# A graph-attention kernel: one-hot transposes folded into the gather matmul, wider blocks, paired results, and a first block spread by TensorE

## The chip, the cores and the metric

The kernel runs on one core of one Trainium2 chip. The metric is the device time of one execution in microseconds; a profiled execution also gives a span, which is about 2 us shorter than its time. PE is TensorE, DVE is VectorE, ACT is ScalarE, POOL is GpSimd, SP is SyncE, which here only issues memory transfers.

## The reference, cut to what matters

There are 4096 nodes with 64 features, 50000 edges, and 4 heads of 64 outputs.

```python
for h in range(n_heads):
    x_proj[h] = x @ weight[h]
# per edge: score = leaky_relu(x_proj[src].att_src + x_proj[dst].att_dst), slope 0.2
output[h, dst] += np.exp(edge_scores[h, i]) * x_proj[h, src]
# per destination: divide by (sum of exp over its edges + 1e-8)
```

## The kernel before

It first sorts the edges, twice, on DVE, so that the edges of each block of 121 destinations lie together as 16 groups of up to 128. Then it loops over 34 blocks. In each block it builds one-hots of the destination and of the source from broadcast bins, gathers features and scores with one-hot matmuls, transposes the destination one-hots on PE, weighs the features by the exponentials, sums them per destination with matmuls, and projects and divides. Names in the lines below: `bc` is the broadcast bins, `oh` the one-hots, `xps` or `ps` what the gather leaves in PSUM (the memory that matmuls write), `ex` the exponentials, `xs` the copied features, `wv` the weights, `val` the weighted features, `acc` the sums, `aT` their copy, `pf` the projection, `inv` and `res` the division. The parts that the change touches:

```python
BD = 121
...
def gather(self, b):                       # per group t of 16
    T.matmul(out=o, lhsT=oh[:, 1, e], rhs=xa[:, 2 * t, :], ...)            # 72 columns
    T.matmul(out=o, lhsT=oh[:, 2, e], rhs=xa[:, 2 * t + 1, :], ...)        # 72 columns
    T.matmul(out=o[:, Din:XC], lhsT=oh[:, 0, e], rhs=adb[:, b, :], ...)    # 8 columns
    ...
    S.activation(out=ex, in_=xps, func=ACTF.Exp);  S.copy(out=xs[:], in_=xps[:, :, 0:Din])

def turn(self, b):                         # 16 transposes and two copies
    T.transpose(out=sp[:, i, :], in_=oh[:, 0, t * W2:(t + 1) * W2], identity=identb[:])
    S.copy(out=Sb[:, q * NT // 2:(q + 1) * NT // 2, :], in_=sp[:])

def run(self):
    ...
    for b in range(ND):
        self.load(b + 3)                   # 1 MB of broadcast bins, SP queue
        self.weigh(b, ...)                 # DVE: wv, val
        self.gather(b + 1)
        self.turn(b + 1)
        self.onehot(b + 2)                 # DVE
        if b:
            self.sink.give(b - 1)          # PE: project; DVE: inv, res; SP: store
        self.scatter(b)                    # PE: 16 + 32 sums
...
win.unpack(0, nc.sync, nc.scalar)          # DVE: bins of 8 blocks; stored to memory
for b in range(3):
    blocks.load(b)                         # and read back, broadcast
for i in range(1, NI):
    win.unpack(i, nc.scalar, nc.scalar)
blocks.run()
```

## Time and profile before

| stage of the profiled execution (span 314.9 us) | us |
|---|---|
| start to the first unpack instruction (sorts, mostly DVE) | 0 to 121.99 |
| first block: unpack, memory, one-hots, gather | 121.99 to 138.01 |
| first val to last val, 33 steps, 4.93 each in the mean | 138.01 to 300.61 |
| last val to the end of the last res | 300.61 to 306.67 |
| to the end (last stores land) | 306.67 to 314.9 |

The median of the first runs was 317.16 us. Two conventions for reading: one *val* instruction is one block, so the distance between starts of consecutive vals is the loop's period; and the name in square brackets behind a line is what the profile takes to have ended the idle time before it. That name is inferred.

### The profile page before, as it was taken

How to read it: one execution, taken by the hardware profiler on the slowest of the kernel's cores; microseconds unless marked ns; L12 is line 12 of the kernel's file. 1: busy time of each engine (PE TensorE's matmuls, PEld its weight loads, DVE VectorE, ACT ScalarE, POOL GpSimd, SP SyncE). 2: the span in 40 equal slices, each digit the busy share in tenths (PEclk: the TensorE clock that was granted, in tenths of full speed). 3: DMA queues.
4: the chain of work that ended last, by engine and by line, in shares of the span. 5: the costliest groups of instructions: out<-in, count | busy, mean ns of one | idle time of the engine just before them, and what ended most of it. 6: DMA issues, size and time to landing. Idle time of an engine off the chain costs nothing. (4 is left out here: it accounts for less than half of the span.)

```text
span 314.9 us, 9697 instructions
## 1 busy us (share of the span) xinstructions
PE 207.2 (66%) x4122; PEld 202.2 (64%) x4122; DVE 275.9 (88%) x552; ACT 172.9 (55%) x324; POOL 18.6 (6%) x40
## 2 busy tenths in 40 slices
PE   0049999000000000099999999999999999999970
PEld 0027999000000000099999999999999999999970
DVE  8999999993999995479999999999999999999960
ACT  3984000000999600067777768677686767768640
POOL 6800000002000005000000000000000000000000
PEclk9999555555555555579999999999999999999996
DMA  7200000002000002991865857667575766667110
GB/s 206 46 1 0 2 0 0 1 0 67 1 0 0 0 28 51 300 395 32 284 234 224 290 191 271 216 237 251 204 276 191 258 228 253 232 227 272 56 38 21
DMA packets 13551, 43.97 MB, mean 140 GB/s; under 512 B 3308, under 2 KB 8492, under 8 KB 9148
## 3 DMA queue, kind: packets, MB, share of 16 engines
q1 hardware_dynamic: 11332, 41.92, 37.7%
q10 hardware_dynamic: 1464, 0.70, 0.8%
q0 software_dynamic: 704, 0.66, 0.8%
q8 instruction: 34, 0.56, 0.8%
q14 instruction: 17, 0.14, 0.2%
HBM read 38.22 MB, written 5.05 MB: 137 GB/s over the span
## 5 line engine op out<-in xcount | busy, mean ns | idle before, releaser
L449 DVE TENSOR_TENSOR val<-xs,wv 128x4096 bf16<-128x4096 bf16 (+1 forms) x35 | 78.0, 2231 | 4.1 <-ACT xs L423 0.7
L437 ACT COPY Sb<-sp 128x1024 bf16<-128x1024 bf16 x68 | 66.3, 1039 | 0.0
L413 PE MATMUL xps<-xa,oh 128*128 128x72 bf16 x544 | 54.1, 194 | 14.5 <-DVE oh L401 14.5
L463 PE MATMUL acc<-Sb,val 128*128 128x121 bf16 x1088 | 63.6, 217 | 0.0
L413 PEld LDWEIGHTS <-oh 128*128 128x128 bf16 x544 | 50.4, 98 | 13.9 <-DVE oh L400 13.9
L463 PEld LDWEIGHTS <-val 128*128 128x128 bf16 x1088 | 58.5, 98 | 0.1
L415 PE MATMUL xps<-xa,oh 128*128 128x72 bf16 x544 | 53.7, 195 | 0.1
L417 PE MATMUL xps<-adb,oh 128*128 128x8 bf16 x544 | 52.8, 169 | 0.0
L415 PEld LDWEIGHTS <-oh 128*128 128x128 bf16 x544 | 49.4, 96 | 1.2 <-DVE oh L401 1.1
L417 PEld LDWEIGHTS <-oh 128*128 128x128 bf16 x544 | 50.1, 97 | 0.0
L400 DVE TENSOR_SCALAR oh<-bc,pF 128x4096 bf16<-128x4096 bf16 x34 | 43.5, 1281 | 4.6 <-DMA bc<-gat_bins 4.6
L420 ACT ACTIVATE ex<-xps 128x256 bf16<-128x256 f32 x34 | 13.4, 395 | 58.3 <-PE xps L417 58.3
L188 DVE TENSOR_TENSOR sA<-sB 128x256 f32<-128x256 f32 (+2 forms) x108 | 39.6, 408 | 1.8
L250 ACT ACTIVATE junk<-kr,nb 128x512 f32<-128x512 f32 x34 | 24.5, 722 | 25.6 <-DVE kr L301 24.5
L188 DVE TENSOR_TENSOR sB<-sA 128x256 f32<-128x256 f32 (+2 forms) x100 | 36.7, 408 | 1.7
L261 PE MATMUL cnt_ps<-sgn,sel 128*128 128x17 f32 (+1 forms) x6 | 1.7, 390 | 53.1 <-ACT sgn L253 53.1
L436 PE MATMUL sp<-identb,oh 128*128 128x128 bf16 x544 | 36.5, 221 | 0.0
L261 PEld LDWEIGHTS cnt_ps<-sgn,sel 128*128 128x128 f32 x6 | 1.4, 318 | 53.2 <-issue 53.2
L423 ACT CAST xs<-xps 128x1024 bf16<-128x1024 f32 x34 | 34.1, 1003 | 0.0
L436 PEld LDWEIGHTS <-oh 128*128 128x128 bf16 x544 | 31.4, 99 | 0.0
L401 DVE TENSOR_SCALAR oh<-bc,pF 128x2048 bf16<-128x2048 bf16 x34 | 25.4, 747 | 0.0
L345 PEld LDWEIGHTS at_ps<-uv,xT 64*128 64x128 f32 x132 | 25.1, 297 | 0.4 <-issue 0.4
(116 smaller groups left out, 255.7 us busy)
## 6 DMA issues: line engine op xcount, KB each, us to landing
bc<-gat_bins SPq DMA_DIRECT2D x34, 1024.0 KB
out_dram<-res SPq DMA_DIRECT2D x33, 121.0 KB
gat_sorted<-sA SPq DMA_DIRECT2D x2, 256.0 KB
eS<-in_edge_index_dram SPq DMA_DIRECT2D x1, 390.0 KB
eD<-in_edge_index_dram ACTq DMA_DIRECT2D x1, 390.0 KB
gat_bins<-tb ACTq DMA_DIRECT2D x9, 32.0 KB
out_dram<-res SPq DMA_DIRECT2D x1, 103.0 KB
win<-gat_sorted,wi POOLq DMA_INDIRECT x5, 2.6
```

The source lines that it names most:

```text
L188: V.tensor_tensor(out=av(d[:], o, [2 * h, n], [1, h]), in0=av(s[:], 0, [2 * h, n], [1, h]), in1=av(s[:], h, [2 * h, n], [1, h]), op=op)
L345: T.matmul(out=ps[:, b, :], lhsT=xT[:, b * step:b * step + P], rhs=uv[:, k, :], start=(b == 0), stop=True, skip_group_check=True)
L400: V.tensor_scalar(out=oh[:, 0:2, :], in0=bc[:], scalar1=pF[:, 0:1], scalar2=None, op0=OP.is_equal)
L401: V.tensor_scalar(out=oh[:, 2, :], in0=bc[:, 1, :], scalar1=pF[:, 1:2], scalar2=None, op0=OP.is_equal)
L413: T.matmul(out=o, lhsT=oh[:, 1, e], rhs=xa[:, 2 * t, :], start=(t % 4 == 0), stop=False, skip_group_check=True)
L415: T.matmul(out=o, lhsT=oh[:, 2, e], rhs=xa[:, 2 * t + 1, :], start=False, stop=False, skip_group_check=True)
L417: T.matmul(out=o[:, Din:XC], lhsT=oh[:, 0, e], rhs=adb[:, b, :], start=False, stop=True, skip_group_check=True)
L423: S.copy(out=xs[:], in_=xps[:, :, 0:Din])
L436: T.transpose(out=sp[:, i, :], in_=oh[:, 0, t * W2:(t + 1) * W2], identity=identb[:])
L437: S.copy(out=Sb[:, q * NT // 2:(q + 1) * NT // 2, :], in_=sp[:])
L449: V.tensor_tensor(out=av(val[:], h * Dout, [Dout, n], [C, NT], [1, Din]), in0=av(xs[:], 0, [0, n], [2, NT * Din // 2], [1, 2]), in1=av(wv[ ...
L463: T.matmul(out=acc[:, k * BD:(k + 1) * BD], lhsT=val[:, t, k * P:(k + 1) * P], rhs=Sb[:, t, 0:BD], start=False, stop=(t == NT - 1), skip_g ...
```

## The change

The intent is to relieve both full engines of the loop and to shorten the gap before it. The 16 transposes go: the third gather matmul gets the identity beside the scores as its moving side, so that it also delivers the turned one-hot, and the gather is done in three chunks (6, 6 and 4 groups) in two PSUM buffers. Blocks grow to 125 destinations, so 33 instead of 34. Epsilon is added by three tiny matmuls. Results are projected per block but divided and stored for two blocks at a time. The first block's bins are spread over the partitions by PE rather than through memory, and groups 3 and 4 are unpacked later.

```diff
-BD = 121
+BD = 125
-    eps = cst.tile([P, 1], F32)
-    V.memset(eps[:], 1e-8)
+    V.memset(e0[:], 1e-8)
+    V.memset(one[:], 1.0)
+    V.memset(nil[:], 0.0)
+    for i in range(3):                     # epsilon in three bf16 parts
+        V.tensor_copy(out=eps[:, i, :], in_=e0[:])
+        if i < 2:
+            V.tensor_copy(out=e1[:], in_=eps[:, i, :])
+            V.tensor_tensor(out=e0[:], in0=e0[:], in1=e1[:], op=OP.subtract)
 ... (cut: identity copied into adb, table layout)
+        def spread(self, b, tb): ...       # PE broadcasts the bins; ACT, ACT, DVE copy them out
-        def turn(self, b): ...
 ... (cut: gather(b, c) of one chunk:)
-                T.matmul(out=o[:, Din:XC], lhsT=oh[:, 0, e], rhs=adb[:, b, :], ...)
+                T.matmul(out=ps[:, i, 0:S0], lhsT=oh[:, 0, e], rhs=adb[:, b, :], ...)   # 136 columns
+            S.activation(out=..., in_=..., func=ACTF.Exp)
+            copy(out=xs[:, t0:t0 + n, 0:P + XC], in_=ps[:, 0:n, 0:P + XC])
 ... (cut: run)
                 self.load(b + 3)
                 self.weigh(b, 2 if b == ND - 1 else 1)
-                self.gather(b + 1)
-                self.turn(b + 1)
+                self.gather(b + 1, 0)
                 self.onehot(b + 2)
                 if b:
-                    self.sink.give(b - 1)
-                self.scatter(b)
+                    self.sink.project(b - 1)
+                    if b % 2 == 0:
+                        self.sink.give(b - 2, 2)     # inv, res and two stores
+                self.sums(b, -1)
+                self.gather(b + 1, 1)
+                self.sums(b, 0)
+                self.gather(b + 1, 2)
+                self.sums(b, 1)
 ... (cut: start)
-        for b in range(3):
+        for i in (1, 2):
+            win.unpack(i, nc.sync, nc.sync)
+        blocks.spread(0, win.tb[:, 0])
+        for b in range(1, 3):
             blocks.load(b)
-        for i in range(1, NI):
-            win.unpack(i, nc.scalar, nc.scalar)
-        blocks.run()
+        blocks.run([lambda i=i: win.unpack(i, nc.sync, nc.sync) for i in range(3, NI)])
```

More of the change, by code (lines that the diff above doesn't have):

```diff
@@ L110 @@
     pm8 = bits("pm8", 0, 7)
-    eps = cst.tile([P, 1], F32)
-    V.memset(eps[:], 1e-8)
+    e0 = cst.tile([1, H], F32)
+    e1 = cst.tile([1, H], F32)
+    eps = cst.tile([1, 3, H], BF16)
+    one = cst.tile([1, P], BF16)
+    nil = cst.tile([1, 3, H], BF16)
+    V.memset(e0[:], 1e-8)
[6 more added lines that the diff above has]
+            V.tensor_tensor(out=e0[:], in0=e0[:], in1=e1[:], op=OP.subtract)
     goff = cst.tile([P, 1], F32)
@@ L150 @@
     xa = cst.tile([P, NB, XC], BF16)
-    adb = cst.tile([P, ND, 2 * H], BF16)
+    AB = P + 2 * H
+    adb = cst.tile([P, ND, AB], BF16)
     Wbd = cst.tile([P, 2, P], F32)
@@ L333, in tables @@
             S.copy(out=uv[:, :, 2 * i:2 * i + 2], in_=av(ps2[:], 0, [2, 2], [1, 2]))
-        S.copy(out=xa[:, :, 0:Din], in_=xf[:])
+        S.copy(out=xa[:, :, 2 * H:XC], in_=xf[:])
         xT = pr.tile([Din, ND * BD + P - BD], F32)
@@ L341, in tables @@
             S.copy(out=xT[:, 4 * q * P:4 * (q + 1) * P], in_=ps[:])
-        for k, (n, step, to) in enumerate(((NB, P, xa[:, :, Din:XC]), (ND, BD, adb[:]))):
+        for k, (n, step, to) in enumerate(((NB, P, xa[:, :, 0:2 * H]), (ND, BD, adb[:, :, P:AB]))):
             ps = pp1.tile([P, n, H], F32, name=f"at_ps{k}")
@@ L348, in tables @@
             S.mul(out=to[:, :, H:2 * H], in_=ps[:], mul=ALPHA)
+        S.copy(out=adb[:, :, 0:P], in_=av(identb[:], 0, [0, ND], [1, P]))
     NT = NR
@@ L374, in unpack @@
                               in_=self.tb[:, i, k, :])
+    CH = ((0, 6), (6, 6), (12, 4))
+    S0 = P + 2 * H
+    XW = 256
     class Blocks:
@@ L382, in __init__ @@
             self.bp = pool(name="blk", bufs=2)
-            self.psx = pool(name="ps_x", bufs=1, space=PSUM)
-            self.pss = pool(name="ps_s", bufs=2, space=PSUM)
+            self.psx = pool(name="ps_x", bufs=2, space=PSUM)
             self.psa = pool(name="ps_a", bufs=1, space=PSUM)
             self.sink = sink
-            self.bc, self.oh, self.xps, self.ex, self.xs, self.wv, self.Sb, self.val = ({} for _ in range(8))
+            self.bc, self.oh, self.ex, self.xs, self.wv, self.val = ({} for _ in range(6))
         def load(self, b):
@@ L394, in load, with spread, onehot, gather @@
                 self.bc[b] = t
-        def onehot(self, b):
-            if b < ND:
-                bc = self.bc.pop(b)
-                oh = self.bp.tile([P, 3, NT * W2], BF16, name="oh")
-                V.tensor_scalar(out=oh[:, 0:2, :], in0=bc[:], scalar1=pF[:, 0:1], scalar2=None, op0=OP.is_equal)
-                V.tensor_scalar(out=oh[:, 2, :], in0=bc[:, 1, :], scalar1=pF[:, 1:2], scalar2=None, op0=OP.is_equal)
-                self.oh[b] = oh
-        def gather(self, b):
+        def spread(self, b, tb):
+            bc = self.bcp.tile([P, 2, NT * W2], BF16, name="bc")
+            for c, (t0, n) in enumerate(CH):
+                ps = self.psx.tile([P, CH[0][1], XW], F32, name="ps")
+                for i in range(n):
+                    T.matmul(out=ps[:, i, :], lhsT=av(identb[:], b * NT + t0 + i, [0, P]), rhs=tb, start=(i % 2 == 0),
+                             stop=True, skip_group_check=True)
+                (S.copy if c < 2 else V.tensor_copy)(out=av(bc[:], t0 * W2, [W2, n], [NT * W2, 2], [1, W2]),
+                                                     in_=av(ps[:], 0, [XW, n], [W2, 2], [1, W2]))
+                if c == 1:
+                    self.onehot(b, bc, *CH[0])
+            for c in (1, 2):
+                self.onehot(b, bc, *CH[c])
+        def onehot(self, b, bc=None, t0=0, nt=NT):
+            if b < ND:
+                if bc is None:
+                    bc = self.bc.pop(b)
+                if t0 == 0:
+                    self.oh[b] = self.bp.tile([P, 3, NT * W2], BF16, name="oh")
+                oh = self.oh[b]
+                e = slice(t0 * W2, (t0 + nt) * W2)
+                V.tensor_scalar(out=oh[:, 0:2, e], in0=bc[:, :, e], scalar1=pF[:, 0:1], scalar2=None, op0=OP.is_equal)
+                V.tensor_scalar(out=oh[:, 2, e], in0=bc[:, 1, e], scalar1=pF[:, 1:2], scalar2=None, op0=OP.is_equal)
+        def gather(self, b, c, copy=S.copy):
             if b >= ND:
@@ L408, in gather @@
             oh = self.oh[b]
-            xps = self.psx.tile([P, NT, P], F32, name="xps")
-            for t in range(NT):
-                o = xps[:, t, 0:XC]
+            if c == 0:
+                self.ex[b] = self.bp.tile([P, 2, H, NT, 2], BF16, name="ex")
+                self.xs[b] = self.bp.tile([P, NT, XW], BF16, name="xs")
+            ex, xs = self.ex[b], self.xs[b]
+            t0, n = CH[c]
+            ps = self.psx.tile([P, CH[0][1], XW], F32, name="ps")
+            for i in range(n):
+                t = t0 + i
@@ L412, in gather @@
                 e = slice(t * W2, (t + 1) * W2)
-                T.matmul(out=o, lhsT=oh[:, 1, e], rhs=xa[:, 2 * t, :], start=(t % 4 == 0), stop=False,
+                T.matmul(out=ps[:, i, P:P + XC], lhsT=oh[:, 1, e], rhs=xa[:, 2 * t, :], start=(i % 2 == 0), stop=False,
                          skip_group_check=True)
-                T.matmul(out=o, lhsT=oh[:, 2, e], rhs=xa[:, 2 * t + 1, :], start=False, stop=False,
+                T.matmul(out=ps[:, i, P:P + XC], lhsT=oh[:, 2, e], rhs=xa[:, 2 * t + 1, :], start=False, stop=False,
@@ L416, in gather @@
                          skip_group_check=True)
-                T.matmul(out=o[:, Din:XC], lhsT=oh[:, 0, e], rhs=adb[:, b, :], start=False, stop=True,
+                T.matmul(out=ps[:, i, 0:S0], lhsT=oh[:, 0, e], rhs=adb[:, b, :], start=False, stop=True,
                          skip_group_check=True)
-            ex = self.bp.tile([P, 2, H, NT, 2], BF16, name="ex")
-            S.activation(out=av(ex[:], 0, [2, NT], [2 * NT, 2 * H], [1, 2]),
-                         in_=av(xps[:], Din, [P, NT], [1, 2 * H], [0, 2]), func=ACTF.Exp)
@@ L422, in gather @@
-            xs = self.bp.tile([P, NT, Din], BF16, name="xs")
-            S.copy(out=xs[:], in_=xps[:, :, 0:Din])
-            self.ex[b], self.xs[b] = ex, xs
-        def turn(self, b):
-            if b >= ND:
-                return
-            oh = self.oh.pop(b)
-            Sb = self.bp.tile([P, NT, W2], BF16, name="Sb")
-            for q in range(2):
-                sp = self.pss.tile([P, NT // 2, W2], BF16, name="sp")
-                for i in range(NT // 2):
-                    t = q * NT // 2 + i
-                    T.transpose(out=sp[:, i, :], in_=oh[:, 0, t * W2:(t + 1) * W2], identity=identb[:])
-                S.copy(out=Sb[:, q * NT // 2:(q + 1) * NT // 2, :], in_=sp[:])
-            self.Sb[b] = Sb
+            S.activation(out=av(ex[:], 2 * t0, [2, n], [2 * NT, 2 * H], [1, 2]),
+                         in_=av(ps[:], P, [XW, n], [1, 2 * H], [0, 2]), func=ACTF.Exp)
@@ L440, in weigh @@
+            copy(out=xs[:, t0:t0 + n, 0:P + XC], in_=ps[:, 0:n, 0:P + XC])
+            if c == len(CH) - 1:
+                self.oh.pop(b)
         def weigh(self, b, parts=1):
-            xs, ex = self.xs.pop(b), self.ex.pop(b)
+            xs, ex = self.xs[b], self.ex.pop(b)
             wv = self.bp.tile([P, H, NT, 2], BF16, name="wv")
@@ L449, in weigh @@
                 V.tensor_tensor(out=av(val[:], h * Dout, [Dout, n], [C, NT], [1, Din]),
-                                in0=av(xs[:], 0, [0, n], [2, NT * Din // 2], [1, 2]),
+                                in0=av(xs[:], S0, [0, n], [XW, NT], [1, Din]),
                                 in1=av(wv[:], h * 2 * NT, [2, n * NT], [0, Din // 2], [1, 2]), op=OP.mult)
             self.val[b] = val
-        def scatter(self, b):
-            val, wv, Sb = self.val.pop(b), self.wv.pop(b), self.Sb.pop(b)
-            acc = self.psa.tile([P, AW], F32, name="acc")
-            for t in range(NT):
-                T.matmul(out=acc[:, 2 * BD:AW], lhsT=Sb[:, t, :], rhs=av(wv[:], 2 * t, [2 * NT, H]), start=(t == 0),
-                         stop=(t == NT - 1), skip_group_check=True)
-            for k in range(2):
-                for t in range(NT):
-                    T.matmul(out=acc[:, k * BD:(k + 1) * BD], lhsT=val[:, t, k * P:(k + 1) * P], rhs=Sb[:, t, 0:BD],
-                             start=False, stop=(t == NT - 1), skip_group_check=True)
-            self.sink.take(b, acc[:])
@@ L467, in run, with sums @@
-        def run(self):
-            self.onehot(0)
-            self.gather(0)
-            self.turn(0)
+        def sums(self, b, k):
+            xs = self.xs[b]
+            if k < 0:
+                self.acc = self.psa.tile([P, AW], F32, name="acc")
+                wv = self.wv.pop(b)
+                for i in range(3):
+                    T.matmul(out=self.acc[:, 2 * BD:AW], lhsT=one[:], rhs=self.sink.first[:, i, :], start=(i == 0),
+                             stop=False, skip_group_check=True)
+                for t in range(NT):
+                    T.matmul(out=self.acc[:, 2 * BD:AW], lhsT=xs[:, t, 0:P],
+                             rhs=av(wv[:], 2 * t, [2 * NT, H]), start=False, stop=(t == NT - 1), skip_group_check=True)
+                return
+            val = self.val[b]
+            for t in range(NT):
+                T.matmul(out=self.acc[:, k * BD:(k + 1) * BD], lhsT=val[:, t, k * P:(k + 1) * P],
+                         rhs=xs[:, t, 0:BD], start=False, stop=(t == NT - 1), skip_group_check=True)
+            if k == 1:
+                self.val.pop(b), self.xs.pop(b)
+                self.sink.take(b, self.acc[:])
@@ L471, in run @@
+        def run(self, also=()):
+            for c in range(len(CH)):
+                self.gather(0, c, V.tensor_copy if c == 1 else S.copy)
+            for f in also[:1]:
+                f()
             self.onehot(1)
+            for f in also[1:]:
+                f()
             for b in range(ND):
@@ L474, in run @@
                 self.weigh(b, 2 if b == ND - 1 else 1)
-                self.gather(b + 1)
-                self.turn(b + 1)
+                self.gather(b + 1, 0)
                 self.onehot(b + 2)
                 if b:
-                    self.sink.give(b - 1)
-                self.scatter(b)
-            self.sink.give(ND - 1)
+                    self.sink.project(b - 1)
+                    if b % 2 == 0:
+                        self.sink.give(b - 2, 2)
+                self.sums(b, -1)
@@ L483 @@
+                self.gather(b + 1, 1)
+                self.sums(b, 0)
+                self.gather(b + 1, 2)
+                self.sums(b, 1)
+            self.sink.project(ND - 1)
+            n = 2 - ND % 2
+            self.sink.give(ND - n, n)
     class Finish:
         def __init__(self, ctx):
+            self.first = eps
             self.fp = ctx.enter_context(tc.tile_pool(name="fin", bufs=2))
             self.psf = ctx.enter_context(tc.tile_pool(name="ps_f", bufs=1, space=PSUM))
-            self.aT = {}
@@ L491, in take @@
         def take(self, b, acc):
-            aT = self.fp.tile([P, AW], F32, name="aT")
-            S.copy(out=aT[:, 0:2 * BD], in_=acc[:, 0:2 * BD])
-            S.activation(out=aT[:, 2 * BD:AW], in_=acc[:, 2 * BD:AW], func=ACTF.Identity, bias=eps[:, 0:1])
-            self.aT[b] = aT
-        def give(self, b):
-            aT = self.aT.pop(b)
-            pf = self.psf.tile([P, C], F32, name="pf")
-            for k in range(2):
-                T.matmul(out=pf[0:BD, k * P:(k + 1) * P], lhsT=aT[:, k * BD:(k + 1) * BD], rhs=Wbd[:, k, :],
-                         start=(k == 0), stop=True, skip_group_check=True)
-            inv = self.fp.tile([P, H], F32, name="inv")
-            V.reciprocal(out=inv[:], in_=aT[:, 2 * BD:AW])
-            res = self.fp.tile([P, H, Dout], F32, name="res")
-            V.tensor_tensor(out=res[0:BD], in0=av(pf[0:BD], 0, [Dout, H], [1, Dout]),
-                            in1=av(inv[0:BD], 0, [1, H], [0, Dout]), op=OP.mult)
-            n = min(BD, N - b * BD)
-            nc.sync.dma_start(out=out[b * BD:b * BD + n, :], in_=res[0:n].rearrange("p h o -> p (h o)"))
+            if b % 2 == 0:
+                self.aT = self.fp.tile([P, 2, AW], F32, name="aT")
+                self.pf = self.psf.tile([P, 2, C], F32, name="pf")
@@ new lines, in take, with project, give @@
+            S.copy(out=self.aT[:, b % 2, :], in_=acc)
+        def project(self, b):
+            for k in range(2):
+                T.matmul(out=self.pf[0:BD, b % 2, k * P:(k + 1) * P], lhsT=self.aT[:, b % 2, k * BD:(k + 1) * BD],
+                         rhs=Wbd[:, k, :], start=(b % 2 == 0 and k == 0), stop=True, skip_group_check=True)
+        def give(self, b, n):
+            inv = self.fp.tile([P, 2, H], F32, name="inv")
+            V.reciprocal(out=inv[0:BD, 0:n], in_=self.aT[0:BD, 0:n, 2 * BD:AW])
+            res = self.fp.tile([P, 2, H, Dout], F32, name="res")
+            V.tensor_tensor(out=res[0:BD, 0:n], in0=av(self.pf[0:BD], 0, [Dout, n * H], [1, Dout]),
+                            in1=av(inv[0:BD], 0, [1, n * H], [0, Dout]), op=OP.mult)
+            for i in range(n):
+                m = min(BD, N - (b + i) * BD)
+                nc.sync.dma_start(out=out[(b + i) * BD:(b + i) * BD + m, :],
+                                  in_=res[0:m, i].rearrange("p h o -> p (h o)"))
@@ L511 @@
     class Total:
         def __init__(self, total):
+            self.first = nil
             self.total = total
@@ L518, in take, with project, give @@
             V.tensor_tensor(out=self.total[:, b, :], in0=acc, in1=self.total[:, b, :], op=OP.add)
-        def give(self, b):
+        def project(self, b):
+            pass
+        def give(self, b, n):
             pass
@@ L590 @@
                             blocks.load(b)
+                        blocks.onehot(0)
                         blocks.run()
             with ExitStack() as st:
+                V.tensor_scalar(out=total[:, :, 2 * BD:AW], in0=total[:, :, 2 * BD:AW], scalar1=1e-8, scalar2=None,
+                                op0=OP.add)
                 fin = Finish(st)
@@ L595 @@
                     fin.take(b, total[:, b, :])
-                    fin.give(b)
+                    fin.project(b)
+                    if b % 2 or b == ND - 1:
+                        fin.give(b - b % 2, b % 2 + 1)
 _INS = ['x', 'edge_index', 'weight', 'att_src', 'att_dst']
```

## The prediction

> **What bounds the kernel now.** First the slices of the page, which split the span of 314.9 us into stages:
>
> ```profile
> PE   0049999000000000099999999999999999999970
> DVE  8999999993999995479999999999999999999960
> ACT  3984000000999600067777768677686767768640
> ```
>
> A slice is 7.87 us. Up to 119 us the VectorE (DVE) sorts almost alone; a short gap follows; from 134 us a loop over 34 blocks fills both TensorE (PE) and DVE; ScalarE (ACT) has slack (36.6 us busy of 50). So three places need reading: the loop's period, the gap before it, and the prologue of the sort.
>
> The loop, in the chain that ended last (start us, duration us):
>
> ```profile
> 248.40 0.91 PE sp L436 x16
> 249.31 0.49 PE pf L501 x4
> 249.79 0.40 PE acc L459 x16
> 250.19 1.72 PE acc L463 x32
> 253.38 0.91 PE sp L436 x16
> ```
>
> Transposes start 4.98 us apart, so that is the period. Between 251.91 and 253.38 stands the gather, 1.47 us. PE's work per block is 0.91 + 0.49 + 0.40 + 1.72 + 1.47 = 4.99 us: the chain is all PE. But DVE's timeline over the same kind of period shows no idle time at all:
>
> ```profile
> 252.59 2.29 DVE L449 TENSOR_TENSOR val<-xs,wv 128x4096 bf16<-128x4096 bf16 x1
> 254.80 1.28 DVE L400 TENSOR_SCALAR oh<-bc,pF 128x4096 bf16<-128x4096 bf16 x1
> 256.00 0.75 DVE L401 TENSOR_SCALAR oh<-bc,pF 128x2048 bf16<-128x2048 bf16 x1
> 256.66 0.17 DVE L504 RECIPROCAL inv<-aT 128x4 f32<-128x4 f32 x1
> 256.92 0.42 DVE L506 TENSOR_TENSOR res<-pf,inv 121x256 f32<-121x256 f32 x1
> 257.26 0.21 DVE L444 TENSOR_TENSOR wv<-ex 128x128 bf16<-128x128 bf16 x1
> 257.58 2.29 DVE L449 TENSOR_TENSOR val<-xs,wv 128x4096 bf16<-128x4096 bf16 x1
> ```
>
> From start to start: val 2.21, the one-hots 1.20 and 0.66, inv 0.26, res 0.34, wv 0.32; sum 4.99. Two engines are full at once. Relieving one alone gains nothing.
>
> The gap before the loop, and the prologue (DVE timeline):
>
> ```profile
> 3.96 0.06 DVE L112 MEMSET eps<- 128x1 f32 x1
> ...
> 5.32 0.39 DVE L548 TENSOR_SCALAR sli<-eS 128x391 int32<-128x391 int32 x1
> ...
> 122.70 0.30 DVE L371 CAST tb<-t 128x256 bf16<-128x256 int32 x1
> ...
> 131.85 1.29 DVE L400 TENSOR_SCALAR oh<-bc,pF 128x4096 bf16<-128x4096 bf16 x1 [3.68 <-DMA bc<-gat_bins]
> ...
> 138.01 2.29 DVE L449 TENSOR_TENSOR val<-xs,wv 128x4096 bf16<-128x4096 bf16 x1 [0.68 <-ACT xs L423]
> ```
>
> The first block's bins are ready at 123.00 but come back broadcast from memory only at 131.8. And the first ScalarE instruction that needs the edge list starts at 5.30, DVE's first at 5.32, with no idle mark before it: DVE's prologue ends just as the edges land, so anything added there delays the whole sort.
>
> **What the Trainium skill says.** "TensorE: Matmul & The Clock Gate", section "Back-to-back issue gap", gives N/2.4 + 2.5 ns for a warm matmul and a floor near 25 ns. The trace agrees: 32 matmuls of N=121 in 1.72 us are 54 ns each (52.9 by the formula), 16 of N=4 in 0.40 us are 25 ns. The same page, "Step-by-step: what each phase is for", says that matmuls stay in program order; my argument rests on this. "VectorE: DVE Perf Modes", section "The perf-mode tier table", gives bf16 tensor_tensor 1224 ns for 2048 elements and fp32 out of PSUM one element per cycle; the trace has 1222 ns for the 2048-element halves of val. "ScalarE: Activation LUTs", section "What ACT_TABLE_LOAD costs", gives 0.833 ns per element; here copies of 242 and 1024 elements take 361 and 1003 ns, which is 0.821 ns, so I use that.
>
> **The change part by part.**
>
> PE per block. Removed: 16 transposes, 0.91. Their work joins the third gather matmul, whose moving side grows from 8 to 136 columns: by the formula 59 ns, against 1.47 us/48 = 30.6 ns now, so 16 x 29 = +0.46. Wider blocks (125 against 121 columns) add 32 x 1.7 ns = 0.05; three tiny matmuls carry epsilon, 0.08. New PE sum: 4.99 - 0.91 + 0.46 + 0.05 + 0.08 = 4.67.
>
> DVE per block. val, both one-hots and wv keep their shapes and stay in their fast modes: 2.21 + 1.20 + 0.66 + 0.32 = 4.39. inv and res are done once for two blocks: 0.26 + 0.34 + 256/0.96 ns = 0.87. So periods alternate between 4.39 and 5.26, mean 4.83.
>
> ACT per block. Three chunks: exponentials of 96, 96, 64 elements and copies of 1200, 1200, 800. From 395 ns for 256 and 1003 ns for 1024 at 0.821 ns per element: 0.26, 0.26, 0.24 and 1.15, 1.15, 0.82, plus 0.37 for the accumulator: 4.25, less 0.1 overlap for each of seven, 3.55. ACT stays under the period.
>
> Number of blocks: 4096/125 rounds up to 33 instead of 34.
>
> The new chain. The last gather chunk of block b+1 now stands on PE behind the first half of block b's sums, and that half needs val of b. val of b+1 in turn needs ACT's copy of that last chunk. So from val to val: val 2.29; DVE to PE 0.05 (the one-hot ending at 296.65 released PE at 296.70); 16 sums of 54.6 ns, 0.87; four triples of 30.2+30.2+59, 0.48; the last matmul's pipeline beyond its slot 0.17 (modelled durations of 0.17 to 0.22 us against slots of 0.03 to 0.06); PE to ACT 0.04; the exponential until the copy can start 0.13; the copy 0.82; ACT to DVE 0.04. Sum 4.89. In periods with res DVE's 5.26 rules; in periods without it 4.89 rules, not 4.39. Mean about 5.08 against 4.98 now.
>
> Loop from the first val to the last: before, 138.01 to 300.61, 162.6 us for 33 steps. After, 32 steps, 15 with res: 15 x 5.26 + 17 x 4.89 = 162.0. The saved block is paid back by longer periods.
>
> Start. The spread works from 123.0: six cold matmuls of 256 columns (slices before the loop show a clock of 0.5, so 213 ns) 1.28; ACT copy of 1536 elements 1.43, twice, to 127.4; DVE one-hots of chunk 0 by 127.0 (from 1281 ns for 4096 and 747 ns for 2048 elements: 0.26 ns per element plus 213 ns); DVE copies chunk 2, to 128.4, then one-hots of chunks 1 and 2, to 130.0; gather chunk 1 on a cold PE from 129.35 to 131.05, its copy on DVE to 132.8; unpack of group 3 (1.0) to 133.8; one-hot of block 1, whose load now stands behind five stores of about 0.72 us and lands near 127.4 + 5.9 = 133.3, to 135.75; unpack of group 4 to 136.75; val near 137.1. That is 0.9 earlier than 138.01, although the first one-hot comes 5.7 earlier: DVE's gaps are filled by pieces and moved unpacks.
>
> Prologue. Nine more tiny DVE instructions net: seven in a dependent row at 0.19 (that spacing stands between the casts at 1.01 and 1.20), three memsets about 0.2, less 0.04: +1.5, all on the path.
>
> Tail. Before, last val to last res end is 306.67 - 300.61 = 6.06. After: second half of val 2.36, second half of sums 0.06 + 0.87 + 0.21, accumulator copy 0.37, projection 0.06 + 0.7, res 0.45: 5.1, so -0.95. The broadcast of the identity into the score table (4224 elements, 3.6 us on ACT) falls where ACT idles 24.5 us and costs nothing.
>
> Sum: +1.5 - 0.9 - 0.6 - 0.95 = about -1.0, so 317.2 becomes 316.2.
>
> **Rivals.** (1) The chain through ACT does not bind, and the loop runs at DVE's 4.83. For: DVE is full now and its work falls. Against: program order on PE. It would make 17 steps 0.5 shorter, -8.5: near 308. (2) The PSUM double buffer or ACT holds the gather. For: three-bank chunks, only two buffers, six evacuations per block on one queue. Against: by my schedule each buffer is free 0.4 us or more before it is wanted, and ACT idles before chunk 2. If it did bind by 0.2 us a block, 323. (3) The start gains in full what the loads cost, 5 us, because unpacks slip into waits: near 312. Against: DVE's queue in the listing of instructions, where both unpacks stand before the first val. (4) The prologue hides behind the edge load: -1.5, near 315. Against: 5.30 and 5.32.
>
> **Range and chances.** Known durations carry most terms. The chain is uncertain by 0.1 x 17 = 1.7, the start by 1.5, res periods by 1. That gives 316 with 312 to 320. Below 310.8 needs rival 1 in most periods: 0.14. Above 323.5 needs an unseen wait in every block: 0.05. Otherwise 0.81.
>
> **What would show it.** Right: periods alternating near 5.26 and 4.89; DVE idle before val, or before wv just ahead of it, released by ACT, about 0.5 us in every other block; PE idle about 0.3 us before sums; sli starting near 6.8; first val near 138.6. Wrong: DVE without idle time in the loop (rival 1), gather matmuls released by ACT (rival 2), or a gather triple that costs far from 119 ns.

## The result, and the profile after

The changed kernel takes 320.88 us in the median of 4 runs (320.01 to 321.31) against 316.99 us (316.63 to 317.96). The ratio is 1.0114, with a 95% interval of 1.0082 to 1.0146: slower by about 1%, where 0.3% faster was predicted, and 0.9 us above the range. A ratio is the mean time of one kernel's fast runs over that of the other's fast runs in the same rounds, so it is not quite the ratio of the medians. The profiled span is 317.9 us.

The busy slices of the page after:

```profile
PE   0039998000000003769999999999999999999981
DVE  7999999993999995698998899889988998999860
```

Both engines now have holes in the loop, where before they were full. On DVE the slices show it; on PE a 9 (90% or more) hides it, but of the 140 us from 150 to 290 PE was busy for 139.92 before and 135.25 after, DVE for 134.22 and 126.83. The page's final chain does not help here: after, its pieces go back only to 300.63, some 4% of the span, so its shares say nothing about the loop. The DVE timeline of two periods shows the holes:

```profile
254.27 2.29 DVE L476 TENSOR_TENSOR val<-xs,wv 128x4096 bf16<-128x4096 bf16 x1 [0.49 <-ACT xs L463]
256.85 1.29 DVE L437 TENSOR_SCALAR oh<-bc,pF 128x4096 bf16<-128x4096 bf16 x1 [0.28 <-PE ps L459]
258.05 0.74 DVE L438 TENSOR_SCALAR oh<-bc,pF 128x2048 bf16<-128x2048 bf16 x1
258.71 0.19 DVE L549 RECIPROCAL inv<-aT 125x8 f32<-125x8 f32 x1
259.00 0.69 DVE L551 TENSOR_TENSOR res<-pf,inv 125x512 f32<-125x512 f32 x1
259.60 0.21 DVE L471 TENSOR_TENSOR wv<-ex 128x128 bf16<-128x128 bf16 x1
259.92 2.29 DVE L476 TENSOR_TENSOR val<-xs,wv 128x4096 bf16<-128x4096 bf16 x1
...
264.83 2.29 DVE L476 TENSOR_TENSOR val<-xs,wv 128x4096 bf16<-128x4096 bf16 x1 [0.49 <-ACT xs L463]
```

The reader sees two different periods. From 254.27 to 259.92 is 5.65 us, the one with res; it contains an idle 0.28 before the one-hots, ended, says the profile, by PE. From 259.92 to 264.83 is 4.91 us, the one without; it contains 0.49 before val, ended by ACT. Over the loop the 15 periods with res take 5.62 us in the mean (5.28 to 6.00), the 17 others 4.91.

The prologue and the start, on DVE:

```profile
7.16 0.30 DVE L599 TENSOR_SCALAR sli<-eS 128x391 int32<-128x391 int32 x1
...
124.18 0.34 DVE L385 CAST tb<-t 128x256 bf16<-128x256 int32 x1
...
128.56 0.62 DVE L437 TENSOR_SCALAR oh<-bc,pF 128x1536 bf16<-128x1536 bf16 x1 [1.28 <-ACT bc L421]
...
133.62 1.41 DVE L463 CAST xs<-ps 128x1200 bf16<-128x1200 f32 x1 [1.25 <-ACT ex L461]
...
138.96 2.29 DVE L476 TENSOR_TENSOR val<-xs,wv 128x4096 bf16<-128x4096 bf16 x1
```

The sort starts at 7.16 instead of 5.32. The first one-hots come at 128.56 instead of 131.85, but the first val at 138.96 instead of 138.01.

So the 3.0 us of span come from here (all from the two DVE timelines, before and after):

| term | predicted | measured |
|---|---|---|
| first val (sum of prologue and start) | +0.6 | 138.96 - 138.01 = +0.95 |
| first val to last val | 162.0 - 162.6 = -0.6 | 167.7 - 162.6 = +5.1 |
| last val to end of last res | -0.95 | 5.10 - 6.06 = -0.96 |
| end of last res to the end | 0 | 6.14 - 8.23 = -2.1 |
| sum | -1.0 | +3.0 |

Nearly the whole miss is one term: 15 periods with res at 5.62 instead of 5.26, which is 15 x 0.36 = 5.4 us. It is 2.1 us milder in the sum because the end of the kernel came out shorter, which I had not foreseen. The packed traces, which also record when each transfer lands, show where: the last store has 103 rows before and 96 after; before, it was issued at 306.70 and landed at 313.05, and after, it was issued at 311.79 and landed by 315.23. Why the one is so much quicker was not tested.

What could hold the one-hots? The list of waits (us in total, times, longest) names two things:

```profile
DVE oh L437 <- DMA bc<-gat_bins: 2.0, 5, 0.6
DVE oh L437 <- PE ps L459: 1.8, 7, 0.3
```

The one-hots need the bins of block b+2, a load of 1 MB. The SP queue in the changed kernel issues these loads in pairs, behind two stores that wait for res:

```profile
249.16 0.68 SPq L555 DMA_DIRECT2D out_dram<-res  x2
249.88 0.83 SPq L409 DMA_DIRECT2D bc<-gat_bins  x2
259.72 0.68 SPq L555 DMA_DIRECT2D out_dram<-res  x2
260.44 0.84 SPq L409 DMA_DIRECT2D bc<-gat_bins  x2
```

And the transfers while one such batch runs (the last columns are PE's granted clock, the mean busy share of the memory engines, and GB/s):

```profile
250.00:251.00 1.00, 1.00 (x33) 0.98 (x32) 1.00 (x1) 0.55 (x1) 0.00 (x0) 1.00 0.61 124
254.00:255.00 1.00, 1.00 (x24) 1.00 (x22) 0.73 (x1) 0.63 (x3) 0.00 (x0) 1.00 1.04 434
256.00:257.00 1.00, 1.00 (x27) 1.00 (x24) 0.72 (x2) 0.39 (x3) 0.00 (x0) 1.00 0.78 311
```

The batch starts slowly, with the stores' small pieces, and runs at 434 GB/s later; two loads and two stores are 2 x 1.05 + 0.26 = 2.35 MB. They are issued from 249.16 and are still moving in the slice 256 to 257, when the one-hots wait until 256.85. In the kernel before, one store and one load alternated every 4.98 us. This suggests a theory: the pairing of results on the in-order SP queue also paired the loads, and one of them lands too late. The expectations below take it to be the second of the pair. The landing records of the packed trace say that it is the first: issued at 249.88, its last part landed at 256.75, and the one-hots began at 256.85; the second landed at 259.52, and its one-hots began at 262.13 without a wait. It is so at all twelve waits: the one-hots begin 0.1 us after the first load of a pair has landed, which is 6.8 to 7.0 us after its issue. In the kernel before, most loads landed 4.5 to 6.2 us after their issue, behind one store. The rival takes the profile's word: PE still reads the one-hot buffer.

A second rival was not tested. A transfer lands in parts, and each leaves a landing record. A store of 125 rows ends in five landing records, one of 121 rows ended in eleven, and the last five of the load's sixteen come late (256.09 to 256.75; the first eleven by 255.01). So the wider blocks may have a share in the lateness, beside the pairing.

### The profile page after: what moved, and what is told of

Same layout as the page of the kernel before. It is cut to its first block, busy times and chain, and to the rows that moved or that the text cites. A ratio compares the mean times of both kernels' runs of the same rounds, so it can differ in the third digit from the quotient of the medians.

```text
span 317.9 us, 8531 instructions
## 1 busy us (share of the span) xinstructions
PE 210.9 (66%) x3591; PEld 196.1 (62%) x3591; DVE 274.4 (86%) x529; ACT 180.7 (57%) x351; POOL 18.7 (6%) x40
## 5 line engine op out<-in xcount | busy, mean ns | idle before, releaser
L463 ACT CAST xs<-ps 128x1200 bf16<-128x1200 f32 (+1 forms) x98 | 101.9, 1040 | 0.0
L459 PE MATMUL ps<-adb,oh 128*128 128x136 bf16 x528 | 78.2, 228 | 0.0
L455 PE MATMUL ps<-xa,oh 128*128 128x72 bf16 x528 | 75.5, 199 | 3.3 <-DVE oh L437 3.0
L457 PE MATMUL ps<-xa,oh 128*128 128x72 bf16 x528 | 75.5, 200 | 0.7 <-DVE oh L438 0.5
L496 PE MATMUL acc<-xs,val 128*128 128x125 bf16 x1056 | 68.8, 218 | 4.8 <-DVE val L476 4.8
L455 PEld LDWEIGHTS <-oh 128*128 128x128 bf16 x528 | 52.8, 100 | 3.5 <-DVE oh L437 3.4
L457 PEld LDWEIGHTS <-oh 128*128 128x128 bf16 x528 | 52.9, 100 | 1.7 <-DVE oh L438 1.6
L461 ACT ACTIVATE ex<-ps 128x96 bf16<-128x96 f32 (+1 forms) x99 | 24.4, 246 | 51.3 <-PE ps L459 49.2
L459 PEld LDWEIGHTS <-oh 128*128 128x128 bf16 x528 | 52.7, 100 | 0.0
L437 DVE TENSOR_SCALAR oh<-bc,pF 128x4096 bf16<-128x4096 bf16 (+2 forms) x35 | 42.8, 1222 | 5.2 <-DMA bc<-gat_bins 2.0
L438 DVE TENSOR_SCALAR oh<-bc,pF 128x2048 bf16<-128x2048 bf16 (+2 forms) x35 | 25.1, 716 | 0.0
L358 PE MATMUL at_ps<-uv,xT 64*128 64x4 f32 x130 | 25.0, 329 | 0.0
L544 PE MATMUL pf<-Wbd,aT 128*125 128x128 f32 x132 | 21.8, 288 | 1.4 <-ACT aT L540 0.9
```

The source lines that it names most:

```text
L358: T.matmul(out=ps[:, b, :], lhsT=xT[:, b * step:b * step + P], rhs=uv[:, k, :], start=(b == 0), stop=True, skip_group_check=True)
L437: V.tensor_scalar(out=oh[:, 0:2, e], in0=bc[:, :, e], scalar1=pF[:, 0:1], scalar2=None, op0=OP.is_equal)
L438: V.tensor_scalar(out=oh[:, 2, e], in0=bc[:, 1, e], scalar1=pF[:, 1:2], scalar2=None, op0=OP.is_equal)
L455: T.matmul(out=ps[:, i, P:P + XC], lhsT=oh[:, 1, e], rhs=xa[:, 2 * t, :], start=(i % 2 == 0), stop=False, skip_group_check=True)
L457: T.matmul(out=ps[:, i, P:P + XC], lhsT=oh[:, 2, e], rhs=xa[:, 2 * t + 1, :], start=False, stop=False, skip_group_check=True)
L459: T.matmul(out=ps[:, i, 0:S0], lhsT=oh[:, 0, e], rhs=adb[:, b, :], start=False, stop=True, skip_group_check=True)
```

## The experiments

Each kernel below is the changed kernel with the edit shown (cut to what matters), unless the text says otherwise. All gave correct results. Ratios are to the kernel before; the changed kernel's own ratio is 1.0114.

**Stores through another queue**

```diff
-                nc.sync.dma_start(out=out[(b + i) * BD:...
+                nc.gpsimd.dma_start(out=out[(b + i) * BD:...
```

> The result stores go through GpSimd's queue, so that the block loads on the SP queue no longer stand behind stores that wait for res. Theory (the wait before the one-hots in periods with res is the late landing of the second of two loads issued together): that wait, 0.34 us in the mean of 15 such periods, goes; those periods fall from 5.62 to about 5.28, the time by about 5 us, to near 315.8. Rival (the one-hots wait for TensorE to leave their buffer, as the profile names TensorE in 7 of 12 waits): no change, about 320.9. A second rival (the memory traffic itself, 1 MB a block, is too slow whatever the order): the wait stays, in other periods.

Measured: 318.77 us, ratio 1.0069 (1.0048 to 1.0091). In the loop the theory held to the hundredth: periods with res 5.282, the others 4.909, and DVE's timeline has no idle before any one-hot of the loop:

```profile
252.82 1.28 DVE L437 TENSOR_SCALAR oh<-bc,pF 128x4096 bf16<-128x4096 bf16 x1
```

The loop became 5.0 us shorter, 162.7. But the total fell by only some 2 us (1.4 by the ratios): from the end of the last res (306.65) to the end of the span (316.8) it now takes 10.1 us instead of 6.1. Only the stores' queue was changed, so that costs it, though from 312 on no memory traffic is left. So the term is confirmed and the remedy is poor. The edit does not tell pairing from the stores' shape: in the other queue these stores end in sixteen landing records, not five.

**Three one-hot buffers**

```diff
-                    self.oh[b] = self.bp.tile([P, 3, NT * W2], BF16, name="oh")      # 2 buffers
+                    self.oh[b] = self.ohp.tile([P, 3, NT * W2], BF16, name="oh")     # 3 buffers
 ... (cut: the pool ohp)
```

> Three buffers for the one-hots instead of two, nothing else. Rival theory (the one-hots wait for a buffer that TensorE still reads): the 12 waits of 0.17 to 0.63 us go, the time falls by about 5 us. Theory of the late load: no change, 320.9 within 0.3%, and the waits stay.

Measured: 319.98 us, ratio 1.0132 (1.0096 to 1.0168), the same as the changed kernel; periods with res 5.56. The waits stayed, and in the list of waits (engine, line, what it waited for: us in total, times, longest) the one-hots of the loop now wait for the load alone:

```profile
DVE oh L438 <- DMA bc<-gat_bins: 2.2, 8, 0.4
```

The rival falls. The name "PE" in 7 of 12 waits of the changed kernel was a coincidence of times: a matmul of the next gather happened to end last before the one-hots began (in the period shown, by its modelled end, at 256.79, against 256.75 for the load).

**Four loads ahead**

```diff
-            self.bcp = pool(name="bc", bufs=3)
+            self.bcp = pool(name="bc", bufs=4)
-                self.load(b + 3)
+                self.load(b + 4)
 ... (cut: blocks 1 to 3, not 1 and 2, are loaded before the loop)
```

> Four buffers for the broadcast bins and each load issued one block earlier; the result stores stay ahead of the loads on the SP queue. Theory (a load lands late because the pair of loads is issued only after the stores of the period before): the wait before the one-hots goes without touching the tail, periods with res fall from 5.62 to 5.28, the others stay at 4.91; the span falls by 5.1 to about 312.8, the time to about 315.8, 0.4% under the kernel before. Rival (the bandwidth of the memory is the bound, 2.25 MB a pair): the pair stays near 10.5 us and the time near 320.9.

Measured: 314.79 us, ratio 0.9928 (0.9890 to 0.9966), span 312.9. Periods 5.281 and 4.913, no idle before a one-hot. The load no longer binds, with the same bytes, the same pairs and the same queue; so bandwidth was not the bound, and the lead of the load was. By the landing records the first load of a pair still lands some 6.9 us after its issue, but now 5 us before it is needed. This is the repaired change: 0.7% faster than the kernel before.

**The last gather chunk before the sums**

```diff
-                self.sums(b, 0)
                 self.gather(b + 1, 2)
+                self.sums(b, 0)
```

> The last gather chunk of the next block stands before the first half of the sums in TensorE's order, so that val of the next block no longer hangs on val of this one. Theory (the chain val, sums, gather, copy, val binds at 4.91 us in the 17 periods without res): the 0.49 us of waiting of val for ScalarE goes, those periods fall to about 4.40, the time by up to 8 us (to 312.5); as the loads then have 10.1 us a pair in place of 10.5, their wait grows, so between 312 and 316. Rival (ScalarE's own queue holds val, whatever TensorE's order): periods stay at 4.9, no change.

Measured: 319.77 us, ratio 1.0107 (1.0059 to 1.0156): no gain. The periods without res did fall, to 4.42 in the steady loop, so the chain from val over the sums and ACT to the next val was real. But the periods with res rose to 6.11 in the mean:

```profile
254.67 2.29 DVE L476 TENSOR_TENSOR val<-xs,wv 128x4096 bf16<-128x4096 bf16 x1
257.91 1.29 DVE L437 TENSOR_SCALAR oh<-bc,pF 128x4096 bf16<-128x4096 bf16 x1 [0.95 <-DMA bc<-gat_bins]
```

The two vals of this period begin at 254.67 and, after it, at 260.99; the wait for the load has grown to 0.95. A pair takes 6.11 + 4.42 = 10.53 us, and 5.62 + 4.91 = 10.53 in the changed kernel. I had expected between 312 and 316, since I took the load's wait for a small addition. It is a closed loop of its own: res, then stores, then loads, then the landing of the first of them, then the one-hots, then the next res. With its 10.5 us a pair it alone set the pace of the changed kernel, and the 0.49 us before val were slack inside it.

**Results one by one**

```diff
                     self.sink.project(b - 1)
-                    if b % 2 == 0:
-                        self.sink.give(b - 2, 2)
+                    self.sink.give(b - 1, 1)
 ... (cut: take, project and the last give handle one block)
```

> Results are finished block by block again, as in the kernel before; all else as changed. Theory: VectorE's sum is 4.39 + 0.26 + 0.34 = 4.99 in every period, above the chain's 4.91, and loads and stores alternate singly, so no late landings: all periods 4.99 to 5.0, 32 of them 159.8 against 167.7 us; the time falls by about 8 us to 313. So the pairing of results, meant to save 0.16 us a block on VectorE, costs time. Rival (the late loads come from the 33 wider blocks or the spread start, not from pairing): waits before the one-hots stay, time above 317.

Measured: 312.27 us, ratio 0.9855 (0.9816 to 0.9894). Almost all periods are 4.98 to 5.00, DVE's full sum (one is 5.88, with a wait of 0.45 for a load), and on the SP queue stores and loads alternate again:

```profile
254.44 0.29 SPq L552 DMA_DIRECT2D out_dram<-res  x1
254.77 0.33 SPq L409 DMA_DIRECT2D bc<-gat_bins  x1
259.42 0.29 SPq L552 DMA_DIRECT2D out_dram<-res  x1
259.76 0.33 SPq L409 DMA_DIRECT2D bc<-gat_bins  x1
```

This undoes one part of the change and gains 8.6 us by the medians (8.2 by the ratios, 7.7 between the profiled spans). The pairing, meant to save 0.16 us a block on DVE, is the part that made the change slower. Late loads are most of that, not all: with four loads ahead a pair of periods takes 5.28 + 4.91 = 10.19, and two single ones 9.98, because the chain holds the short period. Without pairing the rest of the change is 1.45% faster than the kernel before, and the period is the same, 4.99. The one block fewer is not the whole of it. Of the 4.7 us of span (310.2 against 314.9), first val to last val gave 2.1 (160.5 against 162.6, where the kernel before had two short steps, 4.39 and 3.13, at its ends), last val to last res 1.0 and the end after it 2.6; the later first val took 1.0 back.

**Epsilon out of the prologue**

```diff
-    V.memset(e0[:], 1e-8)                  # with the nine instructions after it
 ...
         longest(so2, pp2, ws2, we2, 1)
+        V.memset(e0[:], 1e-8)              # the same ten, while DVE waits for the windows
```

> The ten small VectorE instructions that split epsilon move from the prologue to the 2 us in which VectorE waits for the last window fetch. Theory (the prologue lies bare on the path): the first sort instruction comes back from 7.16 to 5.32, the time falls by 1.8 us, to about 319.1. Rival (the edge load or something behind it takes the place): less than 0.5 us.

Measured: 319.49 us, ratio 1.0093 (1.0072 to 1.0114), not distinguishable from the changed kernel. The sort started at 5.62, 1.54 earlier (now it waited 0.22 for the edges themselves), and the first val came 1.24 earlier, at 137.72. But the second val stood at 143.87, against 143.86 in the changed kernel: the gain was gone after one block. In these microseconds PE's granted clock is 0.50 from 136 to 142 us; in the changed kernel it is back at 1.00 from 142 and at 0.68 in the mean from 140 to 142. Whether the clock took the gain is tested below. These two traces may well overstate the loss: the one here is the slowest of its four executions (320.78; the others 319.02 to 319.67), that of the changed kernel the fastest of its four.

**All three together**

This has four loads ahead, the chunk before the sums, and epsilon moved.

> Four loads ahead, the last gather chunk before the sums, and epsilon moved out of the prologue, all three. Theory: with neither the chain nor the loads binding, VectorE's own sum rules, 4.42 and 5.28, mean 4.83; 32 periods take 155 against 167.7 us, the start gives 0 to 1.2 us more; the time falls by 12 to 14 us to 307 to 309, some 2.5 to 3% under the kernel before. Rival (with shorter periods the memory traffic of 2.25 MB per 9.7 us or ScalarE takes over): pair above 10.2 us, time above 313.

Measured: 308.94 us, ratio 0.9755 (0.9715 to 0.9796), span 307.0. The periods are 5.28 and 4.55, a pair 9.83; val still waits 0.26 for ACT in the short periods, where the theory had 4.42. PE's projections show why (start, duration):

```profile
257.12 0.65 PE L536 MATMUL pf<-Wbd,aT 128*125 128x128 f32 x4
...
262.03 0.65 PE L536 MATMUL pf<-Wbd,aT 128*125 128x128 f32 x4
```

They are 4.91 us apart, and PE is busy for 140.00 of the 140 us from 150 to 290: PE now binds, and the page gives it 54% of the final chain. My sum for PE was 4.67. From start to start this period has 0.58 for the projection, 0.16 for epsilon, 0.43 for the sums of wv, 1.98 for the gathers and 1.76 for the sums of val: 4.91. I had put 0.49, 0.08, 0.40, 1.93 and 1.77. So the projection and epsilon are most of the difference. The gathers' part is that a triple (72, 72 and 136 columns) starts every 124 to 125 ns, where I had put 119 to 121.

**Matmuls that keep the clock**

The first kernel is the previous one again, as a partner on the same chip; the second adds this:

```diff
+            idle = self.psa.tile([P, AW], F32, name="acc")
+            for i in range(64):            # results never read
+                T.matmul(out=idle[:, 0:P], lhsT=identb[:], rhs=identb[:], start=True, stop=True, ...)
             for f in also[:1]:
                 f()
             self.onehot(1)
```

> The kernel with the three changes together once more, as the partner of the next on the same chip. 308.9 within 0.3%.

> The same with 64 matmuls that nobody reads, put where TensorE waits some 3.5 us for the one-hots of block 1. Theory (TensorE's granted clock falls to half in that wait, so that blocks 0 and 1 run on half clock from about 136 to 142.6 us, which took back what moving epsilon had won): the clock stays at 1.0 from 134 on, the second step between vals falls from 5.97 towards 5.3 and the first stays, the time falls by 0.7 to 1.3 us. Rival (the loads of blocks 2 and 3 set the start, whatever the clock): vals stay where they are, no change.

Measured in five rounds: the partner 310.04 us, ratio 0.9763 (0.9732 to 0.9794); with the extra matmuls 308.22 us, ratio 0.9708 (0.9679 to 0.9736). The partner was 0.07% outside its expected band in the median. Busy time per stretch and the granted clock (the column before the last two), first the partner:

```profile
134.00:136.00 2.00, 0.00 (x0) 0.00 (x0) 1.93 (x6) 0.58 (x1) 0.00 (x0) 1.00 1.04 430
138.00:140.00 2.00, 2.00 (x40) 1.83 (x38) 1.90 (x3) 1.07 (x2) 0.00 (x0) 0.50 0.08 20
140.00:142.00 2.00, 2.00 (x28) 2.00 (x27) 2.00 (x3) 1.19 (x3) 0.00 (x0) 0.50 0.79 233
```

With the extra matmuls:

```profile
134.00:136.00 2.00, 2.00 (x37) 2.00 (x36) 1.93 (x6) 0.76 (x2) 0.00 (x0) 0.97 1.00 410
138.00:140.00 2.00, 2.00 (x53) 1.85 (x51) 1.90 (x3) 1.48 (x4) 0.00 (x0) 1.00 0.12 29
140.00:142.00 2.00, 1.51 (x30) 1.35 (x27) 2.00 (x3) 1.97 (x4) 0.00 (x0) 1.00 0.53 209
```

PE idles from 134 to 136 in the partner and then runs blocks 0 and 1 at half clock; with the extra matmuls the clock is 0.97 and then 1.00. The first vals are at the same time (138.47 and 138.51), but the next two steps take 4.39 and 4.84 instead of 4.74 and 6.20: 1.7 us. The medians differ by 1.8 us, more than the 0.7 to 1.3 expected, and the first step fell too, which I had not expected. The two intervals overlap by a little, but the six times of each kernel do not (308.79 to 310.45 against 307.67 to 308.42). This also shows the mechanism that can swallow an earlier start, as in the epsilon experiment: a half clock in the first blocks costs more than a microsecond. That it took the gain there is argued and not shown. This is the fastest kernel, 2.9% under the kernel before.

**The first block through memory again**

```diff
-        for i in (1, 2):
-            win.unpack(i, nc.sync, nc.sync)
-        blocks.spread(0, win.tb[:, 0])
-        for b in range(1, 3):
+        for b in range(3):
             blocks.load(b)
-        blocks.run([...])
+        for i in range(1, NI):
+            win.unpack(i, nc.scalar, nc.scalar)
+        blocks.onehot(0)
+        blocks.run()
```

> The first block's bins come back through memory as in the kernel before, and all groups are unpacked before the loop; the rest as changed. Theory (the spread start won only 0.5 us up to the first val, since VectorE's pieces and moved unpacks fill its gaps): the first val starts 0.5 us later, 139.5, and the time is within 1.5 us of the changed kernel, 321 to 322. Rival (the spread start is worth the whole 5 us of the load): 325 or more.

Measured: 324.68 us, ratio 1.0240 (1.0196 to 1.0283), between the two theories; the first val at 141.87. The trace showed a fault of the experiment: DVE's copy of the second gather chunk, which with the spread waits 1.25 us, here waits 3.60 us for ACT and stands before the one-hots of block 1. So I took it out, with all three copies of the first gather on ACT:

```diff
-                self.gather(0, c, V.tensor_copy if c == 1 else S.copy)
+                self.gather(0, c)
```

> The changed kernel with the bins of the first block back through memory, all groups unpacked before the loop, and all three copies of the first gather on ScalarE, so that nothing stands before VectorE's one-hots of block 1 (in the earlier version of this experiment VectorE's copy of the second chunk stood there). Theory (the spread by itself is worth little, the misplaced copy made most of the 3.8 us): first val near 139.2, time 320 to 322. Rival (the spread is worth 3 us or more): 323.5 or more.

Measured: 320.99 us, ratio 1.0121 (1.0081 to 1.0161), as the changed kernel; span 318.6 against 317.9; first val 139.84 against 138.96. The spread brings the first val 0.9 us forward and moves the total by no more than the noise.

## Why the prediction was wrong, and where it was right

- **The step that failed** is "In periods with res DVE's 5.26 rules". DVE's work was right: where loads don't bind, these periods measured 5.28 in three kernels. But the prediction never asked when the loads of the loop land. The first load of each pair, issued behind two stores, landed only after DVE was ready for it, and the wait, 0.34 us in the mean, made these periods 5.62. Stores through another queue and four loads ahead each removed exactly this; a third one-hot buffer did not. How much of the lateness is the pair's order on the queue, and how much the shape of 125-row stores, is open. No rival named it, and none of the signs of being wrong covered it. It could have been read from the order of instructions on SP (two stores, two loads) and from the kernel before, where one-hots wait once for their load in the loop, 0.34 us: the lead was already thin.
- **The chain** of 4.89 through sums, gather, ACT and val was right in size (4.91), and it does bind once the loads have lead, as the four-load kernel shows. In the changed kernel itself it was slack: breaking it gained nothing. Of the signs of being right, val's 0.49 of waiting for ACT in every other period and PE's 0.3 before sums came as said.
- **Rival 1** (DVE alone sets the pace) needed both bounds removed, and then PE came first at 4.91 a block. PE's sum was under-sized by 0.24, mostly in the projection and epsilon, and by 0.05 because I took an average of 30.6 ns for matmuls of 72 and of 8 columns as the price of one with 72.
- **Rival 2** (buffers or ACT hold the gather by themselves) did not show: no gather matmul waits for ACT in the list of waits of the loop.
- **Start and prologue**: +1.5 and -0.9 were predicted. The prologue cost 1.84 at the first sort instruction and 1.47 at the first unpack (123.46 against 121.99); the start then gave back 0.52. Rival 3 was rightly given little weight: the spread is worth about 0.9 at the first val.
- **The tail** up to the last res was right (5.10). The 2.1 us after it were not in the sum; by the landing records the last store, of 96 rows instead of 103, landed in 3.4 us instead of 6.4, and what followed it took 0.8 more.
- **The range** was too narrow: it covered errors of the terms in the sum and left nothing for a term that was missing. An unseen wait was thought of only in every block, above 323.5; it came in every second one.

## What to carry to other kernels

When results are batched, look at what else goes through the same in-order queue: here, pairing the stores paired the loads, and a saving of 0.16 us a block on a full engine cost about 8 us in all. When several loops of dependence have nearly the same length (here, per pair of blocks, 10.5 us through stores and loads, 10.2 with DVE's long period and the chain in the short one, 9.8 on PE), breaking a shorter one shows nothing until the longest is gone, so write down the period of each, transfers included. And where the profile names an engine as what ended a wait, check it by giving that engine nothing to hold, as the third buffer did.

## What the Trainium skill lacked or had wrong

- "TensorE: Matmul & The Clock Gate", section "Back-to-back issue gap": its formula for an isolated matmul gives 32.5 + 32.5 + 59.2 = 124 ns for the triple of 72, 72 and 136 columns, and the runs show 124 to 125; my 119 came from misusing a mean of the trace. But the section also says that in a stream with weight loads the formula under-counts at small N (about 81 ns at N=128), and that did not show here: 54 ns at N=121, each with its own weight load.
- The same page, section "What's actually happening", gives about 3.4 us of idling to fall to half clock and about 3.4 us of sustained work to come back, in windows that run free of the kernel. Not wrong, but easily read as 3.4 us from the first matmul. Worked out from the clock column, half clock lasted 3.4 us in the changed kernel (means 0.96 from 136 to 138, 0.50, then 0.68 from 140 to 142) and 6.8 us in the partner kernel (0.68 from 136 to 138, 0.50, 0.50, then 0.61 from 142 to 144), though PE was busy for 2.00 of 2.00 us from 138 on.
- "DMA: Bandwidth & Descriptors", section "Where 436 GB/s comes from", says that loads from memory are bound near 358 GB/s per core by the memory's side, and also calls a measured 425 near the fabric's rate. Here, with one core running, the broadcast loads moved 434 GB/s in a microsecond (254 to 255 in the changed kernel), so 358 did not bind them.
- No page that I used has what stores through GpSimd's queue cost at a kernel's end: 10.1 us from the last res to the end, against 6.1 through SP.
